# Four blocks of a product-key expert layer on one core: each block joins a running stream of the value table

## The chip, the cores and the metric

One core of one Trainium2 chip runs the whole program in one launch. The metric is device time in microseconds, the median of several runs. In what follows TensorE is the matmul engine (PE in the profile, PEld its weight loads), VectorE is DVE, ScalarE is ACT, GpSimd is POOL, and SyncE, which issues most transfers, is SP.

## The reference

One step of a decoder layer: 512 prompt tokens and 8 sample tokens go through two token mixers, then through a channel mixer with 16384 experts. The mixers are not touched by the change. The channel mixer is, for each block of 128 tokens:

```
q = (xb @ wq).reshape(blk, 8, 2, 128)
s = einsum('nhcd,ckd->nhck', q, subkeys)
s1, i1 = top_k(s[:, :, 0], 16);  s2, i2 = top_k(s[:, :, 1], 16)
cand = s1[..., :, None] + s2[..., None, :]
top_s, pos = top_k(cand, 16)
eidx = take_along_axis(i1 * 128 + i2, pos)
g = softmax(top_s)
act = gelu(einsum('nd,nhkd->nhk', xb, u[eidx]))
return einsum('nhk,nhkd->nd', g * act, v[eidx])
```

A token has 8 heads x 16 chosen experts = 128 experts. Each has one row of 1024 float32 numbers in `u` and one in `v`.

## The kernel before

The prompt is cut into four blocks of 128 tokens, here A0 and A1 (first half), B0 and B1 (second half). In the code and in the change's title they are blocks 1 to 4 or, as an index, 0 to 3. A half pass (the loop `for hf in range(2)`) does the mixers, the merge, and `scores`, which computes the scores of its two blocks and of the sample tokens. The channel mixer of A0 and A1 is worked off beside the second half pass, that of B0 and B1 behind it. A block goes through these steps:

- **Selection** (`topk`, `retrieve`, L973 to L1018): per head, VectorE's max, index and replace operations over scores, with small operations on GpSimd and ScalarE.
- **Gather** (`gather`, `gather_dot`, L1097 to L1109): 128 times GpSimd issues an indirect transfer (L1102) of 128 rows of `u`, one for each token, 128x1024; VectorE multiplies it with the tokens and sums along the row (L1108, "the dot"). Then `gelu_w` (L1122) makes the weights S.
- **One-hots** (`w_block`, L1154 to L1183): S becomes a dense matrix WT of 128 tokens x 16384 experts, written as 128 slices. In 32 groups of 4 tokens, VectorE compares (L1164, `ohe`), GpSimd multiplies by S (L1167, `oh`), VectorE may do some columns of that (L1169), ScalarE or VectorE make the second one-hot (L145 with L1174, L1177), TensorE multiplies (L1181, `ps_w`) and ScalarE copies the result into WT (L148). `ONAS` and `PMS` hold, per block, how many of the 4 second one-hots ScalarE makes and how many of the 4 products GpSimd makes.
- **Value stream** (`v_part`, L1273): the value table is read in 128 tiles of 128x1024 (L1275, on SP's queue, 5 buffers). For each tile and block TensorE does two matmuls of 512 columns (L1290), each two records in the trace.

A0 and A1 stream together through all 128 tiles, B0 joins for the last 28 (`JB = 100`) and then has 100 tiles of its own: 228 tile loads. B1 has no WT. Beside B0's own tiles `vg_run` gathers 128 rows of `v` for each of B1's tokens (L1313), and TensorE multiplies them with 32-column weights (L1318). The sample tokens (`sample_peer`, L1329 to L1373) are worked in steps: score load, lists, u rows, v rows. B0's gather is held until B1's selection has reached a given head (`HOLD`). A scheduler that reorders instructions on each engine sets the final order; program order is its starting point.

Of the kernel before, what the change touches and what calls it, by code (L numbers as in the profile page):

```python
# [15 lines left out]
P = 128  # L16
D = 1024
# [16 lines left out]
ONAS, PMS = (1, 4, 1, 0), (3, 2, 4, 4)  # L34
# [20 lines left out]
JH = 64  # L55
# [3 lines left out]
def step_kernel(  # L59
# [70 lines left out]
    def pst(tag):  # L130
        return ps.tile([P, 512], F32, tag=tag, name=f"ps_{tag}", bufs=PB[tag])
# [221 lines left out]
    def project(hf):  # L353
# [10 lines left out]
        xx = opnd(sp if hf else fa, f"x{hf}")  # L364
# [285 lines left out]
    nblk = 2  # L650

# [327 lines left out]
    def retrieve(pools, nb, s, rows, top, i12, eidx, vec=False):  # L979
# [23 lines left out]
        eq = (ring if nb[2] == "g" else sp).tile([P, 32, 16], F32, tag=nb[2], name="tk_eq", bufs=nb[3])[:rows]  # L1003
# [28 lines left out]
    def scores(hf, todo, xx):  # L1032
# [78 lines left out]
    def gather(hf, i):  # L1111
        sel, todo = halves[hf]
        d, tok = sel[i], todo[i][0]
        if i == 0 and HOLD[hf] is not None:
            hb, hh = divmod(HOLD[hf], 8)
            with tc.issue_after(sel[hb]["last", hh][HE].ins):
                gather_dot(d, tok, OFF[i])
        else:
            gather_dot(d, tok, OFF[i])
        gelu_w(d["S"], d["g"], d["S"], d["top"], d["e"].bitcast(F32))  # L1120
# [63 lines left out]

    halves = []
    xx, early = project(0), None
    for hf in range(2):
# [67 lines left out]

# [192 lines left out]
```

## Time and profile before

| | |
|---|---|
| Time before, three runs | 2279.82, 2296.55, 2286.86 us; median 2286.86 |
| The profiled execution | 2279.21 us; its span 2277.5 us |
| TensorE's mean granted clock | 0.949 of full speed |
| TensorE, VectorE, ScalarE, GpSimd busy | 92%, 62%, 26%, 58% of the span |
| DMA | 690.15 MB |

Busy is the share of the span in which an engine has an instruction running. The span's axis starts at its first instruction; all stretches are told on it. The second half's scoring fills about 1222 to 1336, A0 and A1 stream from about 1344, B0's one-hots fall in 1650 to 1800, and B0's own tiles with B1's gathered rows in 1930 to 2271.

### The profile page before, as it was taken

The page shows a single profiled execution, that of the slowest core. Times are in us where ns is not written, and L with a number is a line of the kernel's source. Part 1 is how long each engine was busy: PE and PEld are TensorE (multiplying, and loading weights), DVE is VectorE, ACT ScalarE, POOL GpSimd, SP SyncE. Part 2 cuts the span into 40 slices and gives each one's busy share as a digit, 9 for nine tenths or more (in the row PEclk, how much of TensorE's full clock was granted, in tenths as well). Part 3 has the DMA queues.
Part 4 walks back from the last instruction along what each step waited for, and adds up shares of the span by engine and source line. Part 5 has one row for each costly group of instructions (what it writes and reads, how often), then busy time and mean ns, then how long its engine had stood idle before and what let it go on. Part 6 is the DMA issues. An engine that isn't in the chain of part 4 may idle for free.

```text
span 2277.5 us, 26092 instructions
## 1 busy us (share of the span) xinstructions
PE 2098.4 (92%) x8208; PEld 1349.4 (59%) x8208; DVE 1403.7 (62%) x3382; ACT 593.5 (26%) x1615; POOL 1327.5 (58%) x1215
## 2 busy tenths in 40 slices
PE   6999899888999998998988866999999999899998
PEld 4776677777878776787766654444455544222233
DVE  1366675886799878767987989566388775000000
ACT  3334233312345323333423676000022100000000
POOL 0588773553586546667786778444278776555510
PEclk9999999989989999999998866999999999999999
DMA  5687676888799798999987147999699899999988
GB/s 161 198 269 236 229 239 229 282 297 287 243 329 324 269 321 321 337 369 313 318 311 245 43 167 248 410 409 409 252 365 355 320 403 362 410 407 409 409 332 284
DMA packets 293757, 690.15 MB, mean 303 GB/s; under 512 B 31054, under 2 KB 157066, under 8 KB 293618
## 3 DMA queue, kind: packets, MB, share of 16 engines
q0 software_dynamic: 112896, 411.09, 48.7%
q1 hardware_dynamic: 180722, 277.38, 35.1%
q8 instruction: 65, 1.06, 0.2%
q14 instruction: 74, 0.61, 0.1%
HBM read 670.19 MB, written 18.18 MB: 302 GB/s over the span
## 4 chain that ended last, share of the span: by engine, by line
PE 44%; DVE 11%; DMA 10%; issue 7%; POOL 5%; ACT 1%; DVEq 0%; POOLq 0%; ACTq 0%
PE y L1290 20%; PE ps_mm L288 9%; DMA vslab<-in_peer_v,vg_eT 6%; DVE urow L1108 3%; POOL urow L1102 3%; PE ps_mm L293 3%; PE y L1318 3%; PE ps_s L738 2%; DMA urow<-in_peer_u,k_e 1%; PE ps_w L1181 1%; POOL oh L1167 1%; PE ps_s L741 1%; DVE tk_w L975 1%; DVE ohe L1164 1%; DMA vpage<-in_cache_v,kidx 1%
## 5 line engine op out<-in xcount | busy, mean ns | idle before, releaser
L1102 POOL DMA_INDIRECT urow<-in_peer_u,k_e x512 | 632.2, 1235 | 326.9 <-DVE urow L1108 223.3
L1108 DVE SCALAR_TENSOR_TENSOR urow<-urow,xn 128x1024 f32<-128x1024 f32 x512 | 651.2, 1284 | 151.4 <-DMA urow<-in_peer_u,k_e 145.7
L1290 PE MATMUL y<-vtile,WT 128*128 128x512 f32 x1536 | 680.6, 598 | 3.0 <-DMA vtile<-in_peer_v 2.1
L1290 PEld LDWEIGHTS y<-vtile,WT 128*128 128x128 f32 x1536 | 286.6, 191 | 382.5 <-issue 377.8
L288 PE MATMUL ps_mm<-x,wch 128*128 128x264 f32 (+1 forms) x1536 | 385.9, 405 | 25.1 <-DVE sig L312 17.2
L288 PEld LDWEIGHTS ps_mm<-x,wch 128*128 128x128 f32 x1536 | 302.0, 201 | 81.5 <-DVE sig L312 20.7
L831 POOL TENSOR_TENSOR kpage<-kpage,qb 128x1024 f32<-128x1024 f32 x64 | 150.0, 2356 | 73.8 <-DMA qb<-scr_q 65.2
L288 PE MATMUL ps_mm<-hT,wch 128*128 128x256 f32 (+1 forms) x768 | 185.1, 391 | 0.7 <-DMA wch<-in_w_branch_b 0.5
L1313 POOL DMA_INDIRECT vslab<-in_peer_v,vg_eT x128 | 122.2, 955 | 106.2 <-DMA vslab<-in_peer_v,vg_eT 47.7
L1326 DVE TENSOR_TENSOR x1r<-x1r,y 128x512 f32<-128x512 f32 x8 | 5.2, 684 | 249.1 <-DMA x1r<-scr_x 238.3
L288 PEld LDWEIGHTS ps_mm<-hT,wch 128*128 128x128 f32 x768 | 144.4, 194 | 23.5 <-issue 1.3
L293 PE MATMUL ps_mm<-wch,x 128*128 128x256 f32 (+1 forms) x640 | 151.2, 388 | 0.3 <-DVE kS L690 0.3
L1318 PE MATMUL y<-vslab 128*32 128x512 f32 x512 | 138.6, 601 | 12.2 <-DMA vslab<-in_peer_v,vg_eT 12.2
L819 POOL DMA_INDIRECT vpage<-in_cache_v,kidx x64 | 79.8, 1248 | 106.6 <-DVE vacc L897 63.7
L1181 PE MATMUL ps_w<-oh,oh 128*128 128x128 f32 x512 | 88.3, 336 | 46.0 <-POOL oh L1167 29.2
L293 PEld LDWEIGHTS ps_mm<-wch,x 128*128 128x128 f32 (+1 forms) x640 | 108.3, 175 | 30.5 <-issue 2.8
L897 DVE SCALAR_TENSOR_TENSOR vacc<-vpage,aS,vacc 128x128 f32<-128x128 f32 x384 | 110.6, 359 | 19.4 <-DMA vpage<-in_cache_v,kidx 19.3
L1181 PEld LDWEIGHTS ps_w<-oh,oh 128*128 128x128 f32 x512 | 81.4, 242 | 62.3 <-POOL oh L1167 45.5
L1167 POOL TENSOR_TENSOR oh<-ohe,T_S 128x384 f32<-128x384 bf16 (+2 forms) x96 | 96.4, 1011 | 12.7 <-ACT T_S L148 5.6
L1318 PEld LDWEIGHTS y<-vslab 128*32 128x32 f32 x512 | 30.7, 109 | 112.0 <-issue 88.5
L832 DVE TENSOR_REDUCE sK<-kpage 128x16 f32<-128x1024 f32 x64 | 77.1, 1210 | 26.3 <-POOL kpage L831 26.2
L145 ACT ACTIVATE k_e<-k_top,zero 128x128 f32<-128x128 f32 x4 | 1.6, 402 | 346.0 <-DVE k_top L1126 346.0
(420 smaller groups left out, 2634.2 us busy)
## 6 DMA issues: line engine op xcount, KB each, us to landing
vtile<-in_peer_v SPq DMA_DIRECT2D x228, 512.0 KB
wch<-in_w_in SPq DMA_DIRECT2D x256, 256.0 KB
wch<-in_peer_wq SPq DMA_DIRECT2D x64, 256.0 KB
wch<-in_w_branch_a SPq DMA_DIRECT2D x32, 256.0 KB
wch<-in_w_branch_b SPq DMA_DIRECT2D x32, 256.0 KB
wch<-in_w_out SPq DMA_DIRECT2D x32, 256.0 KB
urow<-in_peer_u,k_e POOLq DMA_INDIRECT x512, 7.5
qb<-scr_q SPq DMA_DIRECT2D x8, 512.0 KB
```

Of the source, the lines that this page charges most:

```text
L288: nc.tensor.matmul(out, w[:, c0:c0 + m], xk[:, :n], start=(k == 0 and i == 0), stop=(k == KT - 1 and i == len(tt) - 1))
L293: nc.tensor.matmul(out, x[:, k, t0:t0 + m], ch[k // KP][:, k % KP, :n], start=(k == 0), stop=(k == KT - 1))
L819: nc.gpsimd.indirect_dma_start(out=t, out_offset=None, in_=rows, in_offset=bass.IndirectOffsetOnAxis(ap=kidx[:, b * 8 + pg:b * 8 + pg + 1] ...
L831: (nc.vector if KDV and pg % KDV == KDV - 1 else nc.gpsimd).tensor_mul(kt, kt, qb)
L897: nc.vector.scalar_tensor_tensor(acc[:, h, :], vt[:, h, :], wa, acc[:, h, :], op0=ALU.mult, op1=ALU.add)
L1102: nc.gpsimd.indirect_dma_start(out=gt, out_offset=None, in_=u_rows, in_offset=bass.IndirectOffsetOnAxis(ap=d["e"][:, k:k + 1], axis=0))
L1108: d["dot"] = nc.vector.scalar_tensor_tensor(gt, gt, 1.0, xn2, op0=ALU.mult, op1=ALU.mult, accum_out=d["S"][:, k:k + 1])
L1167: nc.gpsimd.tensor_mul(a[:, :PM], e.rearrange("p j t -> p t j")[:, :PM], sb[:, :PM])
L1181: nc.tensor.matmul(pw[:, t, :], b[:, t, :], a[:, t, :], start=True, stop=True)
L1290: nc.tensor.matmul(py[q], lw, rv[:, q * 512:(q + 1) * 512], start=(j == j0 and i == 0), stop=(j == j1 and i == len(pp) - 1))
L1313: nc.gpsimd.indirect_dma_start(out=gt, out_offset=None, in_=v_rows, in_offset=bass.IndirectOffsetOnAxis(ap=eT[:, t:t + 1], axis=0))
L1318: nc.tensor.matmul(py[q][32 * j:32 * j + 32, :], wz[:, t, :], gt[:, q * 512:(q + 1) * 512], start=(i == 0), stop=(i == 31), skip_group_che ...
```

## The change

- A0 streams alone through tiles 0 to 63, beginning inside the second half's scoring. For that the tiles and its accumulators have pools (`values`, `psumo`) that are open from there on, and the operands pool closes early.
- A1 joins for tiles 64 to 127. Then A1 goes on through tiles 0 to 63, B0 joins from tile 16 (`JC`), and goes on alone through tiles 64 to 127 and 0 to 15. That is 272 tile loads.
- `scores(1)` selects for B0 only; B1's selection is `late`, behind A0's one-hots. `HOLD` is not used any more. B0's gather follows.
- The sample block is done whole, between A0's end and B1's gather. Then B1's gather, then B0's one-hots.
- B1's value rows are gathered by expert slot: 128 transfers, one per slot with a row for each token (`v_rows_acc`), and VectorE multiplies each by its weight and adds it to the sum. TensorE's share of it (`vg_prep`, `vg_run`) is gone. The rows use 15 slots in the memory of A1's WT.
- Prompt results are stored from ScalarE's queue, not SP's.
- `ONAS[0]` goes from 1 to 2, `PMS[0]` from 3 to 4 and `PMS[1]` from 2 to 4.

```diff
-ONAS, PMS = (1, 4, 1, 0), (3, 2, 4, 4)
+ONAS, PMS = (2, 4, 1, 0), (4, 4, 4, 4)
-JH = 64
+JH, JC = 64, 16
...
-                if not BF[hf] or d is sel[0]:
+                if hf == 0 or d is sel[0]:
                     topk(d, h)
...
-        if BF[hf]:
+        def late():
             for h in range(8):
                 topk(sel[1], h)
-        for d, (tok, t0, rows, sample) in zip(sel, todo):
-            if not sample:
-                softmax16(tp, d["top"], d["g"], P, 8)
-        return sel
+            softmax16(tp, sel[1]["top"], sel[1]["g"], P, 8)
+        return sel, late
...
+    def v_done(tok, py):
+        t = dv[0].tile([P, D], F32, tag="v", name="x1r", bufs=VB)
+        nc.sync.dma_start(t, scr_x1[tok:tok + P])
+        for q in range(2):
+            nc.vector.tensor_add(t[:, q * 512:(q + 1) * 512], t[:, q * 512:(q + 1) * 512], py[q])
+        nc.scalar.dma_start(y_prompt[0, tok:tok + P], t)
+
+    def v_rows_acc(d, tok, acc, slot):
+        nc.sync.dma_start(acc, scr_x1[tok:tok + P])
+        for k in range(P):
+            gt = slot()
+            nc.gpsimd.indirect_dma_start(out=gt, out_offset=None, in_=v_rows,
+                                         in_offset=bass.IndirectOffsetOnAxis(ap=d["e"][:, k:k + 1], axis=0))
+            nc.vector.scalar_tensor_tensor(acc, gt, d["S"][:, k:k + 1], acc, op0=ALU.mult, op1=ALU.add)
+            yield
+        nc.scalar.dma_start(y_prompt[0, tok:tok + P], acc)
...
         if hf == 1:
+            octx.close()
+            dv[0] = ctx.enter_context(tc.tile_pool(name="values", bufs=1, side="right"))
             gather(0, 0)
             gather(0, 1)
+        sel, late = scores(hf, todo, xx2)
+        halves.append((sel, todo))
...
+            w_block(halves[0][0][0], wA0, wr, pst_w, 0)
+            late()
+            gather(1, 0)
+            useA0 = ([pst("a"), pst("o")], wA0, 0, P - 1)
+            for j in range(JH):
+                v_part(j, [useA0])
...
+    useA1 = (v_acc(1), wA1, JH, JH - 1)
+    for j in range(JH, P):
+        v_part(j, [useA0, useA1])
+    v_done(0, useA0[0])
+    steps = sample_peer()
+    for _ in steps:
+        pass
+    gather(1, 1, lambda: wr.tile([P, P], F32, name="ge_y", bufs=1))
+    wB0 = w_new(wr, wr)
+    w_block(selB[0], wB0, wr, pst_d, 2)
+    useB0 = (v_acc(2), wB0, JC, (JC - 1) % P)
     for j in range(JH):
+        v_part(j, [useA1] + ([useB0] if j >= JC else []))
+    v_done(P, useA1[0])
+    slab = [wt.tile([P, 8, D], F32, tag="WT", name="vslab", bufs=2) for _ in range(2)]
...
-        v_part(j, [useB0], False)
-        if j % 3 == 2:
+    run = v_rows_acc(selB[1], HALF + P, slab[0][:, 0, :], gslot)
+    for j in [*range(JH, P), *range(JC)]:
+        v_part(j, [useB0])
+        with tc.issue_after(selB[1]["rows"].ins):
             next(run, None)
```

VectorE, A1's first one-hots (L1164 before, L1171 after: `ohe`; `T_i` is A1's list). Before, they stand between the selections of the scoring (`tk_`, `k_top`):

```order
1415 L977 MAX_INDEX tk_si<-tk_sv,tk_w 128x8
1416 L973 MAX k_top<-tk_c 128x8
1417 L1164 TENSOR_TENSOR ohe<-iota_8781,T_i_10366 128x512 x3
1418 L1018 SCALAR_TENSOR_TENSOR k_e<-k_i_9320 128x16
1419 L973 MAX tk_sv<-sco 128x8 x2
1420 L1017 TENSOR_REDUCE k_i_9313<-tk_eq 128x2x16
1421 L974 MAX_INDEX tk_p<-k_top,tk_c 128x8
1422 L975 MATCH_REPLACE tk_w<-k_top,tk_c 128x136
1423 L975 MATCH_REPLACE tk_w<-tk_sv,sco 128x128
1424 L1169 TENSOR_TENSOR oh_10380<-ohe,T_S 128x256
```

After, four of them stand in B1's selection, and the next ones behind its last results (`k_i_8800` and `k_e` are B1's; `urow,k_S` are B0's dots):

```order
1470 L1033 TENSOR_TENSOR k_g<-smd,sml 128x128
1471 L1021 TENSOR_REDUCE k_i_8800<-tk_eq 128x2x16
1472 L1022 SCALAR_TENSOR_TENSOR k_e<-k_i_8800 128x16
1473 L1120 SCALAR_TENSOR_TENSOR urow,k_S<-urow,xn_10367 128x1024 x2
1474 L1021 TENSOR_REDUCE k_i_8800<-tk_eq 128x2x16
1475 L1337 MEMSET wz 128x64
1476 L1120 SCALAR_TENSOR_TENSOR urow,k_S<-urow,xn_10367 128x1024
1477 L1022 SCALAR_TENSOR_TENSOR k_e<-k_i_8800 128x16
1478 L1120 SCALAR_TENSOR_TENSOR urow,k_S<-urow,xn_10367 128x1024
1479 L1171 TENSOR_TENSOR ohe<-iota_9496,T_i_11036 128x512 x2
1480 L1120 SCALAR_TENSOR_TENSOR urow,k_S<-urow,xn_10367 128x1024
1481 L1171 TENSOR_TENSOR ohe<-iota_9496,T_i_11036 128x512
```

The fifth one-hot and all later ones have moved behind the end of B1's selection, each beside one dot of B0.

TensorE, B0's one-hots (`ps_w<-oh`) and the stream (`y`). Before, groups stand between stream matmuls:

```order
1347 L1290 MATMUL y_10959<-vtile,WT 128x512
1348 L1290 MATMUL y_10960<-vtile,WT 128x512
1349 L1181 MATMUL ps_w<-oh_12220,oh_12222 128x128 x4
1350 L1181 MATMUL ps_w<-oh_12235,oh_12237 128x128 x4
1351 L1290 MATMUL y_10961<-vtile,WT 128x512
1352 L1290 MATMUL y_10958<-vtile,WT 128x512
1353 L1290 MATMUL y_10959<-vtile,WT 128x512
1354 L1290 MATMUL y_10960<-vtile,WT 128x512
1355 L1290 MATMUL y_10961<-vtile,WT 128x512
1356 L1290 MATMUL y_10958<-vtile,WT 128x512
```

After, the stream's last matmuls of A1 are followed by all 32 groups (8 shown):

```order
1470 L1198 MATMUL y_11596<-vtile,WT 128x512
1471 L1148 MATMUL ps_w<-ident,k_S 128x128
1472 L1198 MATMUL y_11595<-vtile,WT 128x512
1473 L1198 MATMUL y_11596<-vtile,WT 128x512
1474 L1188 MATMUL ps_w<-oh_12566,oh_12568 128x128 x4
1475 L1188 MATMUL ps_w<-oh_12581,oh_12583 128x128 x4
1476 L1188 MATMUL ps_w<-oh_12596,oh_12598 128x128 x4
1477 L1188 MATMUL ps_w<-oh_12611,oh_12613 128x128 x4
1478 L1188 MATMUL ps_w<-oh_12626,oh_12628 128x128 x4
1479 L1188 MATMUL ps_w<-oh_12641,oh_12643 128x128 x4
1480 L1188 MATMUL ps_w<-oh_12656,oh_12658 128x128 x4
1481 L1188 MATMUL ps_w<-oh_12671,oh_12673 128x128 x4
```

The stream matmuls between the groups are gone; the next stream matmul comes after the 32nd group.

SP's queue, the sample's requests (`s`, `scr_g`, `scr_e`, `gT`, `eT`) among the value tiles. Before:

```order
280 L1275 DMA vtile<-in_peer_v 128x1024 x70
281 L1331 DMA s_11743<-scr_s 64x256
282 L1275 DMA vtile<-in_peer_v 128x1024 x3
283 L1099 DMA xn_11805<-scr_xn_59 128x1024
284 L1275 DMA vtile<-in_peer_v 128x1024 x2
285 L1338 DMA scr_g<-s_g 64x16
286 L1275 DMA vtile<-in_peer_v 128x1024
287 L1344 DMA gT<-scr_g 128x8x1
288 L1275 DMA vtile<-in_peer_v 128x1024 x2
289 L1337 DMA scr_e<-s_e 64x16
290 L1275 DMA vtile<-in_peer_v 128x1024 x2
291 L1343 DMA eT<-scr_e 128x8x1
```

After:

```order
297 L1194 DMA vtile<-in_peer_v 128x1024 x97
298 L1311 DMA s_11986<-scr_s 64x256
299 L1194 DMA vtile<-in_peer_v 128x1024 x4
300 L1110 DMA xn_12150<-scr_xn_59 128x1024
301 L1194 DMA vtile<-in_peer_v 128x1024 x2
302 L1318 DMA scr_g<-s_g 64x16
303 L1194 DMA vtile<-in_peer_v 128x1024
304 L1324 DMA gT<-scr_g 128x8x1
305 L1317 DMA scr_e<-s_e 64x16
306 L1202 DMA x1r<-scr_x_58 128x1024
307 L1323 DMA eT<-scr_e 128x8x1
```

The score load `s` has moved from behind the 70th tile load to behind the 121st, and the list `eT` from behind the 80th to behind the 128th. The residual load `x1r` of A0 has come among them.

## Rows read from the trace of the kernel before

**Rows 1.** Page, engines: busy us (share), instructions; DMA total; the value-tile issues.

```profile
PE 2098.4 (92%) x8208; PEld 1349.4 (59%) x8208; DVE 1403.7 (62%) x3382; ACT 593.5 (26%) x1615; POOL 1327.5 (58%) x1215
...
DMA packets 293757, 690.15 MB, mean 303 GB/s; under 512 B 31054, under 2 KB 157066, under 8 KB 293618
...
vtile<-in_peer_v SPq DMA_DIRECT2D x228, 512.0 KB
```

**Rows 2.** Windows: length, then PE, PEld, DVE, ACT, POOL busy (instructions), PEclk, DMA share, GB/s.

```profile
1222.00:1304.00 82.00, 75.47 (x367) 59.97 (x365) 70.24 (x382) 36.55 (x101) 50.44 (x88) 0.96 0.36 120
...
1336.00:1413.00 77.00, 48.09 (x196) 37.54 (x196) 63.49 (x112) 52.61 (x153) 66.44 (x59) 0.63 0.77 267
1413.00:1612.00 199.00, 198.29 (x465) 88.69 (x466) 118.76 (x195) 3.14 (x11) 91.18 (x93) 0.99 1.01 400
...
1672.00:1800.00 128.00, 126.31 (x472) 70.55 (x470) 115.95 (x174) 34.52 (x115) 106.47 (x87) 1.00 0.95 346
...
1930.00:2194.00 264.00, 250.60 (x762) 69.53 (x760) 10.48 (x31) 1.20 (x4) 133.31 (x140) 0.99 1.02 406
```

**Rows 3.** Windows, a stretch inside the first common stream.

```profile
1450.00:1600.00 150.00, 150.00 (x351) 66.43 (x350) 91.16 (x148) 0.00 (x0) 68.46 (x74) 1.00 1.03 409
```

**Rows 4.** Chain that ended last, in order: start us, us, what.

```profile
1425.53 232.88 PE y L1290 x542
...
2194.04 72.31 PE y L1290 x168
2266.37 4.50 DMA x1r<-scr_x
```

**Rows 5.** Timeline of POOL: start us, us, instruction [idle before].

```profile
1336.77 1.56 POOL L1102 DMA_INDIRECT urow<-in_peer_u,k_e  x1 [0.15 <-issue]
1338.64 0.94 POOL L1102 DMA_INDIRECT urow<-in_peer_u,k_e  x1 [0.30 <-issue]
```

**Rows 6.** Groups by form, 1230 to 1345, DVE's selection: busy us, mean ns | idle.

```profile
L976 DVE MAX8 tk_sv<-tk_w 128x8 f32<-128x128 f32 x32 | 8.9, 277 | 0.0
...
L1017 DVE TENSOR_REDUCE k_i<-tk_eq 128x32 f32<-128x512 f32 x15 | 10.0, 666 | 0.0
```

**Rows 7.** Groups by form, 1336 to 1413, A1's one-hots.

```profile
L145 ACT ACTIVATE oh<-iota,T_n 128x128 f32<-128x128 f32 x84 | 26.9, 398 | 0.0
...
L1174 ACT ACTIVATE oh<-oh,one 128x512 f32<-128x512 f32 x23 | 16.1, 716 | 0.1
L148 ACT ACTIVATE WT<-ps_w 128x256 f32<-128x256 f32 x46 | 15.1, 380 | 21.5 <-PE ps_w L1181 21.4
```

**Rows 8.** Groups by form, 1413 to 1612, B0's gather.

```profile
L1108 DVE SCALAR_TENSOR_TENSOR urow<-urow,xn 128x1024 f32<-128x1024 f32 x95 | 116.1, 1225 | 78.4 <-DMA urow<-in_peer_u,k_e 78.4
L1102 POOL DMA_INDIRECT urow<-in_peer_u,k_e x93 | 91.2, 980 | 96.9 <-DVE urow L1108 90.6 <-issue 5.7 <-DVE ohe L1164 0.3
```

**Rows 9.** Groups by form, 1650 to 1805, B0's one-hots beside B1's gather.

```profile
L1108 DVE SCALAR_TENSOR_TENSOR urow<-urow,xn 128x1024 f32<-128x1024 f32 x70 | 92.6, 1351 | 10.5 <-DMA urow<-in_peer_u,k_e 10.3
L1102 POOL DMA_INDIRECT urow<-in_peer_u,k_e x68 | 89.7, 1319 | 25.2 <-DVE urow L1108 14.3 <-issue 8.6 <-DVE oh L1177 1.0
...
L1167 POOL TENSOR_TENSOR oh<-ohe,T_S 128x512 f32<-128x512 bf16 x32 | 34.2, 1081 | 6.2 <-ACT T_S L148 5.6 <-PE ps_w L1181 0.2
...
L1177 DVE TENSOR_TENSOR oh<-iota,T_i 128x384 f32<-128x384 f32 x29 | 27.7, 969 | 2.8 <-PE ps_w L1181 2.6 <-ACT oh L145 0.2
...
L1164 DVE TENSOR_TENSOR ohe<-iota,T_i 128x512 bf16<-128x512 bf16 x29 | 18.0, 628 | 16.6 <-POOL oh L1167 16.6
```

**Rows 10.** Groups by form, 1930 to 2194, B1's gathered value rows.

```profile
L1318 PE MATMUL y<-vslab 128*32 128x512 f32 x512 | 138.6, 601 | 12.2 <-DMA vslab<-in_peer_v,vg_eT 12.2
L1313 POOL DMA_INDIRECT vslab<-in_peer_v,vg_eT x128 | 122.2, 955 | 106.2 <-DMA vslab<-in_peer_v,vg_eT 47.7 <-PE y L1318 22.6 <-issue 20.7
```

**Rows 11.** Timeline of SP's queue, the sample's requests: start us, us, instruction.

```profile
1632.46 0.45 SPq L1331 DMA_DIRECT2D s<-scr_s  x1
...
1666.66 0.43 SPq L1343 DMA_DIRECT2D eT<-scr_e  x1
```

More of the change, by code (lines that the diff above doesn't have):

```diff
@@ L130, in pst @@
     def pst(tag):
-        return ps.tile([P, 512], F32, tag=tag, name=f"ps_{tag}", bufs=PB[tag])
+        return (pso if tag in "ao" else ps).tile([P, 512], F32, tag=tag, name=f"ps_{tag}", bufs=PB[tag])
     def st1(shape, name, dt=F32):
@@ L1054, in score @@
                 for c in range(2):
-                    nc.tensor.matmul(p[:rows, c * P:(c + 1) * P], qts[c][:, t0:t0 + rows], skT[:, c, :],
-                                     start=True, stop=True)
+                    mm = nc.tensor.matmul(p[:rows, c * P:(c + 1) * P], qts[c][:, t0:t0 + rows], skT[:, c, :],
+                                          start=True, stop=True)
+                if d is not None:
+                    d["score"] = mm
                 if sample:
@@ L1109, in gather_dot, with gather @@
                                                           accum_out=d["S"][:, k:k + 1])
-    def gather(hf, i):
+    def gather(hf, i, y=None):
         sel, todo = halves[hf]
         d, tok = sel[i], todo[i][0]
[L1114 to L1120, printed above, removed]
+        gather_dot(d, tok, OFF[i])
+        gelu_w(d["S"], d["g"], d["S"], d["top"], d["e"].bitcast(F32) if y is None else y())
     def gelu_w(s, g, out, t, y):
@@ L1183, in w_block, with v_part @@
                 copy(w[:, :, t0:t0 + TG], pw[:, :, j0:j0 + w.shape[1]].rearrange("p t j -> p j t"))
+    def v_part(j, use):
+        vt = dv[0].tile([P, D], F32, tag="v", name="vtile", bufs=VB)
+        nc.sync.dma_start(vt, v_rows[j * P:(j + 1) * P])
+        for py, wT, j0, j1 in use:
+            w = next(w[:, j - b, :] for w, b in wT if b <= j < b + w.shape[1])
+            for q in range(2):
+                nc.tensor.matmul(py[q], w, vt[:, q * 512:(q + 1) * 512], start=(j == j0), stop=(j == j1))
+    def v_done(tok, py):
+        t = dv[0].tile([P, D], F32, tag="v", name="x1r", bufs=VB)
+        nc.sync.dma_start(t, scr_x1[tok:tok + P])
+        for q in range(2):
+            nc.vector.tensor_add(t[:, q * 512:(q + 1) * 512], t[:, q * 512:(q + 1) * 512], py[q])
[5 more added lines that the diff above has]
+            nc.gpsimd.indirect_dma_start(out=gt, out_offset=None, in_=v_rows,
+                                         in_offset=bass.IndirectOffsetOnAxis(ap=d["e"][:, k:k + 1], axis=0))
+            nc.vector.scalar_tensor_tensor(acc, gt, d["S"][:, k:k + 1], acc, op0=ALU.mult, op1=ALU.add)
+            yield
+        nc.scalar.dma_start(y_prompt[0, tok:tok + P], acc)
     halves = []
@@ L1254, in step_kernel @@
     fctx.close()
+    tctx.close()
     dctx = ExitStack()
```

113 lines of the change are left out of this document (19 added, 94 removed).

## The prediction

> **What bounds the kernel now.** I read the page's engines first [rows 1]. TensorE is busy 92% of the span of 2277.5 us, no other engine over 62%. That is an average, so the windows of the tail come next [rows 2]. Three kinds of stretch show. From 1336 to 1413 TensorE is busy 48.09 of 77 us at a granted clock of 0.63 (of 2.4 GHz): it waits for A1's one-hots. From 1413 to 1612 and in the 150 us of [rows 3] it is full, and the DMA share is 1.01 to 1.03 at 400 to 409 GB/s: engine and memory are both at their limit. From 1930 to 2194 the share is 1.02 again, TensorE busy 250.60 of 264. The chain [rows 4] says the same: 542 records of the value stream in 232.88 us, then 168 in 72.31, 0.43 us each. One block's share of a tile is two matmuls in four records, 1.71 us; two blocks, 3.42 us. A value tile and a gathered row set are each 128x1024 float32, 0.524 MB; at 409 GB/s that is 1.28 us. So a one-block tile with one gathered row costs DMA 2.56 us and TensorE 1.71: that pair is DMA-bound, while two blocks per tile (3.42) cover it.
>
> **The change part by part.** The times below are on the axis of the profiled execution; everything up to the second half's scoring is untouched.
>
> *What TensorE gains and DMA loses.* The 512 records of gathered rows on TensorE go: 138.6 us [rows 10]. The 1536 records of the stream stay. Value tiles go from 228 [rows 1] to 64 + 64 + 64 + 80 = 272: 44 more, 23 MB beside 690 MB, 44 x 1.28 = 56 us at the limit. The 128 v rows stay, loaded by expert slot instead of by token.
>
> *(a) Scoring.* A0's stream starts inside it: the order has about 10 tiles before the last scoring matmul, 10.5 x 1.71 = 18 us on a TensorE that is busy 75.47 of 82 us there [rows 2], so they lengthen it. For block A0 VectorE loses its column of one-hot products and a third of its compares; this may give back 5 us, bounds 0 to 15. Against that the hold is gone which let B0's gather start at 1336.77 [rows 5], where the last tenth or so of B1's selection before that point no longer stands. B0's first row: 1324, bounds 1310 to 1338.
>
> *(b) B1's selection.* In the new order VectorE places only four of A1's 32 first one-hots before the rest of B1's selection. What is left is 6.5 heads. A head is ten operations over 128 columns at 0.277, five over 136 at about 0.29, a reduce at 0.666 [rows 6] and small ones, 6 to 6.4 us: 41 us. With it stand 27 dots of B0, 1.225 to 1.35 us [rows 8, 9] and 0.08 for reading the accumulator: 38. With one-hots and a softmax about 84 us, at 90% filled 93 (the row before has VectorE busy 63.49 of 77 us with a lighter mix). A1's one-hots go on at about 1424, bounds 1395 to 1445. The stream of A0 alone covers TensorE for part of this.
>
> *(c) A1's one-hots.* 28 groups are left. ScalarE per group, by busy time over count [rows 7]: 4 x 0.32 + 0.70 + 2 x 0.33 = 2.64 us, some 2.7 with gaps. GpSimd now multiplies all four columns, 1.08 [rows 9], and issues one row, 0.94 + 0.30 idle [rows 5]: 2.3. ScalarE sets the pace: 28 x 2.7 = 76 to 78, at worst the 3.35 us a group that 23 groups took in those 77 us: 94. A0 and A1 can stream together from 1502, bounds 1470 to 1525. A0's 64 lone tiles have run out by then, so TensorE idles some 45 us.
>
> *(d) A0 and A1 together:* 64 x 3.42 = 219 us, to 1721. DMA needs 64 tiles and some 70 rows, 172 us: hidden.
>
> *(e) The sample block.* Its requests stand in SP's queue behind value tiles. Before, the score load went at 1632.46, behind the 70th tile, and the expert list 34 us later [rows 11], and nothing hung on them. Now they stand behind the 121st and the 128th, and all of the sample's work ends before B0's one-hots begin on TensorE. Tile 121 is let in when tile 116 has been used: 1502 + 52 x 3.42 = 1680; the list 27 later; eight u rows and dots and the gelu another 35 to 40: 1745. TensorE has work meanwhile, 21 tiles of A1 alone (36 us) and the sample's 14, until the transposes for B0 at 1779: 8 us of stall beyond the work, bounds 0 to 30.
>
> *(f) B0's one-hots.* Now 32 groups stand on TensorE with no stream matmul between, so their whole pace is exposed. GpSimd: 32 x 1.08 + 49 rows x 1.4 + about 5 = 108; VectorE: 32 x (0.63 + 0.97) + 49 x 1.43 = 121 at the durations of [rows 9], 98 at uncontended ones. I take 115, as the two engines share the load as they did then, bounds 95 to 135. TensorE does only some 30 us of work in it, DMA only 54 pieces (69 us of 115). B0 streams from 1894. Before, stream matmuls between the groups hid this: from 1672 TensorE was busy 126.31 of 128 us [rows 2].
>
> *(g) The rest.* By then 153 tiles are loaded, so 119 remain, with 69 u rows and 128 v rows: 316 x 1.28 = 405 us, bounds 405 to 420, to 2306. TensorE's need is 91 x 1.71 and 71 x 1.71, 277 us: it is hidden behind DMA. The accumulate on VectorE is not in this trace. Its nearest row is the dot of the same shape, 1.225 us [rows 8]; a row issue is 0.955 [rows 10]. Both lie under 2.56 us per pair, so I add nothing, with a high end in the last rival and none below, since DMA alone sets the low one. How tile and row share the engines decides only which finishes first.
>
> The Trainium skill, "DMA: Bandwidth & Descriptors", section "SWDGE vs HWDGE vs iDMA", says that each DMA engine takes turns between the queues that software and hardware descriptors feed. By that rule tiles and rows would advance one for one and both end together. This trace doesn't settle it, as [rows 10] show row issues waiting for buffers; the total is the same either way.
>
> *(h) Tail.* Before, the chain's last load ended at 2270.87 [rows 4] and the span at 2277.5: the adds and the store took some 6.5 us, and as much is added here. The last store goes out from ScalarE's queue; nothing else is on it by then, 0 to 2 us either way. Early pools, operands in their own pool and own PSUM banks cost no instruction; their price is the waits in (b) and (c).
>
> Sum: 2306 + 6.5 = 2313 of span, and 1.7 around it (2279.21 less 2277.5) gives 2314, 1.5% above 2279.21. The median of the runs, 2286.86, stands 0.3% above the profiled execution; on that scale I say 2318.
>
> A check by bytes: from the first B0 row on there are 400 row sets and 228 tiles before, 628 x 1.28 = 805 us, of 935 that passed; 130 us idle. After: 400 and some 253, 837 us, and idle in (b) to (f) of 37 + 47 + 0 + 46 = 130. The change must find 32 us of DMA idle to break even; it starts only 12 earlier.
>
> **The rivals.**
>
> *Faster: A1's one-hots are not held up.* If VectorE clears B1's selection by 1380, because the topk's waits were TensorE's and ScalarE's and not its own, A0 and A1 join at 1425 instead of 1502, and B0's start falls to about 1817. The end is then 1817 + 405 + 8 = 2230 to 2245, 1.8% faster. For it: A1's one-hots ran to 1413 before, with B1's selection done. Against: selection and dots alone are 79 us of VectorE. It decides when the join comes before about 1445.
>
> *No change.* Every stall in (c), (e) and (f) a little shorter: B0's one-hots at uncontended pace (95 instead of 115), the join at 1487. That is 35 us, ending near 2278. For it: each is inside its own bounds. Against: the contended durations in [rows 9] were measured with the same neighbours.
>
> *Slower by more: the accumulate locks out row issues.* If issue (0.94 + 0.30) and accumulate (1.225) can't overlap, a row costs 2.47 us. When A1's stream ends, about 121 v rows and 75 tiles are left; the rows then take 299 us, where DMA needs 196 x 1.28 = 251 for both: 48 later, 2362. For it: rows issued at 1320 ns beside one-hots and dots [rows 9]. Against: 980 ns beside dots alone [rows 8].
>
> The Trainium skill, "SBUF — State Buffer", section "Who interferes with whom", says that VectorE and GpSimd share a port pair that is locked exclusively. By it this rival would get more weight; the 980 ns of [rows 8] beside 95 dots don't agree with a lock for each row's issue.
>
> **How the numbers follow.** Forecast 0.50, no change 0.26, faster 0.17, slower by more 0.07. A measurement tells about 1% from no change here, 23 us: below 2264 is faster, above 2310 slower. The forecast's own spread (2295 to 2340) gives 0.41 to slower and 0.09 to same; no change gives 0.24 to same, 0.02 to slower. That makes 0.17 faster, 0.33 same, 0.50 slower. The range runs from 2240, in the middle of the faster rival, to 2348; it leaves out half of that rival and the last one. The likeliest case's own range is 2295 to 2340.
>
> **What would show it.** Right: TensorE idle for tens of us before A0 and A1 stream together at about 1500; a stretch of some 115 us near 1780 with the B0 one-hots on TensorE at low clock; then a DMA share of 1.0 to the end, with TensorE waiting for value tiles. Wrong: a join before 1445, one-hots of B0 in under 90 us, or an end stretch where VectorE or GpSimd, not DMA, ends the waits.

## The result, and the profile after

The changed kernel takes 2351.44 us (median of four runs, 2339.56 to 2355.60) against 2291.70 beside it: a ratio of 1.026, 95% interval 1.0211 to 1.0309. It is slower, as forecast, but by 2.6%, where 2318 was named and 2348 was the end of the range. The profiled execution took 2339.56 us, its span 2337.9.

The page of the changed kernel, engines, transfers, the two groups of B1's value rows and the value-tile issues; compare [rows 1] and [rows 10]:

```profile
PE 1982.6 (85%) x7694; PEld 1318.8 (56%) x7694; DVE 1551.5 (66%) x3440; ACT 612.5 (26%) x1647; POOL 1348.2 (58%) x1216
...
DMA packets 300090, 713.16 MB, mean 305 GB/s; under 512 B 31758, under 2 KB 157770, under 8 KB 299954
...
L1213 DVE SCALAR_TENSOR_TENSOR vslab<-vslab,k_S 128x1024 f32<-128x1024 f32 x128 | 164.5, 1285 | 56.8 <-DMA vslab<-in_peer_v,k_e 53.7
L1211 POOL DMA_INDIRECT vslab<-in_peer_v,k_e x128 | 152.2, 1189 | 86.2 <-DMA vslab<-in_peer_v,k_e 53.5
...
vtile<-in_peer_v SPq DMA_DIRECT2D x272, 512.0 KB, 6.8
```

TensorE's work fell by 115.8 us and its share from 92% to 85%. 713.16 - 690.15 = 23.0 MB more are moved: 44 tile loads. The accumulate took 1.285 us a row, as the dots do.

Windows of the changed kernel, the columns as in [rows 2]: up to the join of A0 and A1, the common stream, the sample block, B0's one-hots, B0 with A1, and then three pieces of the end:

```profile
1320.00:1478.00 158.00, 111.81 (x427) 63.67 (x427) 117.06 (x333) 90.03 (x258) 136.46 (x140) 0.87 0.87 315
1478.00:1693.00 215.00, 214.75 (x507) 95.33 (x506) 105.05 (x199) 4.26 (x11) 80.16 (x86) 1.00 0.90 346
1693.00:1766.00 73.00, 59.46 (x120) 18.99 (x119) 17.53 (x41) 1.20 (x4) 22.41 (x21) 0.91 0.93 354
1766.00:1888.00 122.00, 66.53 (x268) 53.81 (x267) 116.80 (x171) 42.95 (x130) 103.03 (x87) 0.60 0.74 234
1901.00:2047.00 146.00, 145.82 (x340) 64.71 (x341) 79.40 (x129) 0.00 (x0) 67.59 (x68) 1.00 1.03 410
2047.00:2180.00 133.00, 103.78 (x209) 35.97 (x207) 76.62 (x69) 1.60 (x4) 77.21 (x56) 0.99 1.03 409
2180.00:2276.00 96.00, 0.00 (x0) 0.00 (x0) 92.96 (x73) 0.00 (x0) 66.50 (x65) 0.51 0.96 377
2276.00:2334.00 58.00, 51.85 (x116) 22.65 (x116) 1.21 (x2) 0.00 (x0) 0.00 (x0) 0.92 0.80 281
```

The common stream fills TensorE (214.75 of 215) but not DMA (0.90). Around the one-hots of B0 neither is full. From 1901 to 2180 DMA is at 409 to 410 GB/s. The row from 2180 is the one to stop at: TensorE is busy 0.00 of 96 us, and there are still value tiles to come, as the last row shows (116 records, 29 tiles).

SP's waits in the last 440 us (engine and line, what it waited for, us in total, times, longest):

```profile
SPq L1194 <- PE y L1198: 253.7, 113, 3.8
SPq L1194 <- DMA out_y_prompt<-vslab: 111.1, 1, 111.1
```

One value-tile load waits 111.1 us for `out_y_prompt<-vslab`, the store of B1's result, which is issued from ScalarE's queue and can only run when the last of 128 rows is accumulated. TensorE's timeline there (start, us, instruction, idle before):

```profile
2172.48 1.98 PE L1198 MATMUL y<-vtile,WT 128*128 128x512 f32 x4 [0.58 <-DMA vtile<-in_peer_v]
...
2177.60 1.98 PE L1198 MATMUL y<-vtile,WT 128*128 128x512 f32 x4 [0.58 <-DMA vtile<-in_peer_v]
2281.58 18.81 PE L1198 MATMUL y<-vtile,WT 128*128 128x512 f32 x39 [102.00 <-DMA vtile<-in_peer_v]
```

Up to 2177.60 a tile comes every 2.56 us. Then TensorE waits 102.00 us for one. VectorE's timeline beside it:

```profile
2175.41 1.28 DVE L1213 SCALAR_TENSOR_TENSOR vslab<-vslab,k_S 128x1024 f32<-128x1024 f32 x1 [1.27 <-DMA vslab<-in_peer_v,k_e]
2177.84 22.42 DVE L1213 SCALAR_TENSOR_TENSOR vslab<-vslab,k_S 128x1024 f32<-128x1024 f32 x17 [1.15 <-DMA vslab<-in_peer_v,k_e]
```

With tiles running it gets one row in 2.56 us; when they stop, its accumulates stand back to back, 17 in 22.42 us, so that now VectorE sets the pace, at 1.32 us a row (busy 92.96 of 96 us). The rows are done at 2275. Then the store goes out, the tiles come back, and 29 of them run alone at TensorE's pace.

Why would a tile load wait for a store from another engine's queue? The program's order, with the semaphores that each instruction waits for, says it (first the store on ScalarE, then tile loads on SP; `...` where rows are left out):

```
1389 L1215 DMA out_y_prompt<-vslab 128x1024 [waits DMAHW7_49,DVE_49]
...
857 L1194 DMA vtile<-in_peer_v 128x1024 [waits DMAHW0_49,PE_49]
858 L1194 DMA vtile<-in_peer_v 128x1024 [waits DMAHW1_49,PE_49]
859 L1194 DMA vtile<-in_peer_v 128x1024 [waits DMAHW7_49,DMAHW2_49,PE_49]
860 L1194 DMA vtile<-in_peer_v 128x1024 [waits DMAHW3_49,PE_49]
```

Transfers issued from SP and from ScalarE signal their end on the same eight semaphores, given out in turn by the scheduler. The store got number 7. The next load to get number 7 is row 859, with 28 more behind it, and it must wait until the store has signalled. No data passes between the two. Transfers issued from GpSimd have eight semaphores of their own.

Two more views answer to rows of before. B0's first u row (timeline of GpSimd) and the sample's score load and list (SP's queue), against [rows 5] and [rows 11]:

```profile
1320.38 1.04 POOL L1113 DMA_INDIRECT urow<-in_peer_u,k_e  x1
```

```profile
1659.19 0.45 SPq L1311 DMA_DIRECT2D s<-scr_s  x1
...
1686.76 0.37 SPq L1323 DMA_DIRECT2D eT<-scr_e  x1
```

And B0's one-hots, groups by form from 1766 to 1888, against [rows 9]:

```profile
L1120 DVE SCALAR_TENSOR_TENSOR urow<-urow,xn 128x1024 f32<-128x1024 f32 x54 | 73.3, 1379 | 0.0
L1113 POOL DMA_INDIRECT urow<-in_peer_u,k_e x55 | 67.7, 1231 | 18.6 <-DVE urow L1120 7.7 <-issue 7.6 <-DVE oh L1184 0.9
...
L1174 POOL TENSOR_TENSOR oh<-ohe,T_S 128x512 f32<-128x512 bf16 x32 | 37.2, 1165 | 0.7
L1184 DVE TENSOR_TENSOR oh<-iota,T_i 128x384 f32<-128x384 f32 x32 | 28.9, 914 | 0.0
L1171 DVE TENSOR_TENSOR ohe<-iota,T_i 128x512 bf16<-128x512 bf16 x32 | 21.8, 689 | 5.7 <-POOL oh L1174 3.8 <-ACT T_i L151 1.9
```

GpSimd's products (1165 ns) and the dots (1379) are a little slower than they were with the same neighbours (1081 and 1351), and GpSimd and VectorE are busy 103 and 117 of the 122 us.

**The balance of transfers.** The stretch from B0's first row to the last value matmul, before and then after:

```profile
1337.00:2271.00 934.00, 888.56 (x2523) 384.28 (x2522) 410.35 (x705) 98.89 (x304) 506.21 (x462) 0.97 0.95 362
```

```profile
1320.00:2334.00 1014.00, 765.71 (x2007) 360.57 (x2006) 613.28 (x1025) 140.71 (x409) 563.92 (x527) 0.87 0.91 344
```

934 us at 362 GB/s are 338 MB, 827 us at the 409 GB/s of [rows 3]; 1014 at 344 are 349 MB, 853 us. So 26 of the 80 us more are transfers, and idle DMA time went from 107 to 161. The same sum over the windows above puts that at 36 us up to the join, 33 in the common stream, 10 beside the sample block, 52 beside B0's one-hots, and 26 from 2180 on. The first four are 131; the prediction had counted 130 for all. The last was not in it.

That balance starts at B0's first row, and by then the changed kernel has already loaded 24 tiles, beside the scoring. From the last residual store ahead of the scoring to the last value matmul, in both kernels, the sums are 357.0 MB in 1083.1 us before and 380.1 MB in 1149.2 after: 56 us more of transfers at 409 GB/s, the price of the 44 loads, and idle DMA time up only from 210 to 220. The early tiles fill DMA time that stood idle, and the new stalls and the store wait take it back.

### The profile page after: what moved, and what is told of

Read it like the earlier page. It is cut to its first block, busy times and chain, and to the rows that moved or that the text cites. A ratio compares the mean times of both kernels' runs of the same rounds, so it can differ in the third digit from the quotient of the medians.

```text
span 2337.9 us, 25323 instructions
## 1 busy us (share of the span) xinstructions
PE 1982.6 (85%) x7694; PEld 1318.8 (56%) x7694; DVE 1551.5 (66%) x3440; ACT 612.5 (26%) x1647; POOL 1348.2 (58%) x1216
## 2 busy tenths in 40 slices
DMA packets 300090, 713.16 MB, mean 305 GB/s; under 512 B 31758, under 2 KB 157770, under 8 KB 299954
## 4 chain that ended last, share of the span: by engine, by line
PE 43%; DVE 15%; DMA 10%; POOL 5%; issue 5%; ACT 1%; POOLq 0%; DVEq 0%; ACTq 0%; SPq 0%
PE y L1198 14%; PE ps_mm L291 10%; DMA vslab<-in_peer_v,k_e 5%; DVE urow L1120 4%; DVE vslab L1213 4%; PE ps_a L1198 3%; PE ps_mm L296 3%; PE ps_o L1198 3%; POOL urow L1113 3%; DMA vtile<-in_peer_v 2%; PE ps_w L1188 1%; DMA vpage<-in_cache_v,kidx 1%; POOL oh L1174 1%; DMA urow<-in_peer_u,k_e 1%; PE ps_s L742 1%
## 5 line engine op out<-in xcount | busy, mean ns | idle before, releaser
L1113 POOL DMA_INDIRECT urow<-in_peer_u,k_e x512 | 600.9, 1174 | 382.5 <-DVE urow L1120 273.6
L1120 DVE SCALAR_TENSOR_TENSOR urow<-urow,xn 128x1024 f32<-128x1024 f32 x512 | 663.1, 1306 | 162.1 <-DMA urow<-in_peer_u,k_e 157.0
L1198 PE MATMUL y<-vtile,WT 128*128 128x512 f32 x1024 | 476.2, 609 | 145.8 <-DMA vtile<-in_peer_v 145.3
L1198 PEld LDWEIGHTS y<-vtile,WT 128*128 128x128 f32 x1024 | 191.9, 193 | 417.3 <-issue 220.7
L1213 DVE SCALAR_TENSOR_TENSOR vslab<-vslab,k_S 128x1024 f32<-128x1024 f32 x128 | 164.5, 1285 | 56.8 <-DMA vslab<-in_peer_v,k_e 53.7
L1211 POOL DMA_INDIRECT vslab<-in_peer_v,k_e x128 | 152.2, 1189 | 86.2 <-DMA vslab<-in_peer_v,k_e 53.5
L1198 PE MATMUL ps_a<-vtile,WT 128*128 128x512 f32 x256 | 134.4, 607 | 2.0 <-DMA vtile<-in_peer_v 1.4
L1198 PE MATMUL ps_o<-vtile,WT 128*128 128x512 f32 x256 | 132.1, 598 | 0.0
L1174 POOL TENSOR_TENSOR oh<-ohe,T_S 128x512 f32<-128x512 bf16 x96 | 109.5, 1147 | 5.3 <-PE ps_w L1188 1.8
L993 POOL TENSOR_TENSOR tk_c<-tk_sv 128x120 f32<-128x120 f32 (+1 forms) x33 | 19.2, 582 | 115.1 <-DVE tk_sv L980 105.2
```

The lines of the kernel that those rows point to most:

```text
L1113: d["rows"] = nc.gpsimd.indirect_dma_start(out=gt, out_offset=None, in_=u_rows, in_offset=bass.IndirectOffsetOnAxis(ap=d["e"][:, k:k + 1], ...
L1120: d["dot"] = nc.vector.scalar_tensor_tensor(gt, gt, 1.0, xn2, op0=ALU.mult, op1=ALU.mult, accum_out=d["S"][:, k:k + 1])
L1174: nc.gpsimd.tensor_mul(a[:, :PM], e.rearrange("p j t -> p t j")[:, :PM], sb[:, :PM])
L1198: nc.tensor.matmul(py[q], w, vt[:, q * 512:(q + 1) * 512], start=(j == j0), stop=(j == j1))
L1211: nc.gpsimd.indirect_dma_start(out=gt, out_offset=None, in_=v_rows, in_offset=bass.IndirectOffsetOnAxis(ap=d["e"][:, k:k + 1], axis=0))
L1213: nc.vector.scalar_tensor_tensor(acc, gt, d["S"][:, k:k + 1], acc, op0=ALU.mult, op1=ALU.add)
```

## The experiments

The part of the program that the change leaves alone varies by up to 34 us between runs: its last residual store came at 1184.8 us in one profile and at 1218.5 in another. So single runs are compared by what is left of the span after that store, called the tail here: 1089.6 us before, 1153.1 after. Each tail is from one profile. In the six kernels that are alike up to B0's stream, that stream begins 702.3 to 705.5 us after the store, so a difference of 3 us or less says nothing.

| kernel | tail, us | ratio to before, 95% interval |
|---|---|---|
| changed | 1153.1 | 1.0260 (1.0211 to 1.0309) |
| store from GpSimd's queue | 1133.4 | 1.0191 (1.0146 to 1.0236) |
| stores from SP's queue | 1155.0 | 1.0265 (1.0223 to 1.0306) |
| store on SP behind the last tile | 1134.2 | one run |
| GpSimd's store, B0 joins at 0 | 1141.9 | 1.0244 (1.0198 to 1.0289) |
| GpSimd's store, B0 joins at 48 | 1150.8 | 1.0264 (1.0217 to 1.0310) |
| GpSimd's store, a quarter of the accumulate | 1130.7 | one run |
| GpSimd's store, half the last tile loads | 1083.2 | one run |
| GpSimd's store, B0's compares on ScalarE | 1155.9 | 1.0304 (1.0253 to 1.0356) |
| before, B1's rows on VectorE | 1076.7 | 0.9908 (0.9875 to 0.9940) |
| the same, with the change's one-hot split | 1069.4 | 0.9937 (0.9904 to 0.9970) |

### The store of B1's rows from GpSimd's queue

```diff
-        nc.scalar.dma_start(y_prompt[0, tok:tok + P], acc)
+        nc.gpsimd.dma_start(y_prompt[0, tok:tok + P], acc)
```

> One edit to the changed kernel: the store of B1's accumulated rows goes out from GpSimd's queue instead of ScalarE's. Theory S (store wait): in the changed kernel's trace one value-tile load on SP waits 111 us for that store, so no tile comes from 2180 to 2276 and 29 tiles at TensorE's 1.71 us are left behind the rows. Without the wait tiles and rows run out together or rows last: at 2180 some 30 tiles and 73 rows are left, 103 x 1.28 = 132 us, end of the stream at about 2312 and a span of about 2317 instead of 2338; no value-tile load waits for a store. Rival R (rest bound by transfers and VectorE whatever the order): the wait only changes which of them is late, span 2333 to 2343.

Measured: a span of 2323.1 and a tail of 1133.4, 19.7 us less than the changed kernel's. Its end in windows:

```profile
1905.00:2051.00 146.00, 145.96 (x340) 64.71 (x341) 79.97 (x131) 0.00 (x0) 69.23 (x68) 1.00 1.03 410
2051.00:2258.00 207.00, 159.98 (x325) 54.93 (x323) 112.88 (x97) 1.60 (x4) 117.02 (x85) 1.00 1.03 409
```

Tiles now run to 2258 at 409 GB/s and the rows alone end it. B0's stream began 705 us after the last residual store in both, so all of the 19.7 lies at the end: that is the store wait, as theory S has it. Whole times agree, but are not clear of noise by themselves: the intervals of the two ratios overlap a little. The span came 6 above the expected 2317, 5 of it from the later start of this run (its last residual store came at 1189.7, against 1184.8).

### All prompt stores from SP's queue

```diff
-        nc.scalar.dma_start(y_prompt[0, tok:tok + P], t)
+        nc.sync.dma_start(y_prompt[0, tok:tok + P], t)
...
-        nc.scalar.dma_start(y_prompt[0, tok:tok + P], acc)
+        nc.sync.dma_start(y_prompt[0, tok:tok + P], acc)
```

> One part of the change undone: all prompt stores go out from SP's queue, as before the change. In the order the store of B1's rows stands 38 tile loads before the end of SP's queue. Theory S: the load behind the store waits for it in the queue itself, so the rows end near 2270 with some 38 to 40 tiles left, 39 x 1.71 = 67 us: span 2340 to 2352, no better than the changed kernel. Rival R: 2333 to 2343. If ScalarE's queue itself were what costs (the idea that the queue is bad), the span would fall to 2315 or less.

Measured: span 2353.8, tail 1155.0. Undoing this part brings nothing back: SP itself now stands at the store for longer, with tile loads behind it.

```profile
SPq L1215 <- DVE vslab L1213: 116.6, 1, 116.6
```

### The store on SP, behind the last tile load

```diff
-        nc.scalar.dma_start(y_prompt[0, tok:tok + P], acc)
+        with tc.issue_after(last_tile_load.ins):
+            nc.sync.dma_start(y_prompt[0, tok:tok + P], acc)
```

> Spans are now counted from the last store of a residual row block ahead of the second half's scoring, since the part before it, which the change leaves alone, varies by 19 us between runs (before: 2277.5 - 1187.9 = 1089.6; changed: 2337.9 - 1184.8 = 1153.1; store from GpSimd's queue: 1133.4). One edit to the changed kernel: the last store goes out from SP's queue, queued behind the last value-tile load. Theory S (a tile load that must wait for that store costs the time, whichever queue it is on): 1130 to 1138. Rival (SP's or ScalarE's hardware queue itself is slower for the store than GpSimd's): 1150 or more.

Measured: 1134.2. The same queue for this store as in the run before, 20.8 us less: it is the place of the store ahead of tile loads that costs, not the queue. (The run before had also moved the other prompt stores to SP; up to B0's stream that changed nothing, 705.5 us against 705.2.) The reading rests on the tail alone: this run's whole time, 2349.36 us, is that of the changed kernel, since its last residual store came 29 us later. B0's stream began 2.9 us earlier after that store than in the changed kernel, so 16 of the 18.9 us lie in the end.

### B0 joins at tile 0, and at tile 48

```diff
-JH, JC = 64, 16
+JH, JC = 64, 0
```

> On top of the store from GpSimd's queue, B0 joins the second pass at tile 0 instead of 16: 256 tile loads instead of 272, 8.4 MB less, and 16 lone tiles of A1 (27 us of TensorE) less ahead of B0's one-hots. Theory B (transfers bind from A0's end on): 16 x 1.28 = 20 us less, as far as no more DMA idle time comes: span 2295 to 2305. Rival C (what binds is TensorE without cover while the sample block and B0's one-hots are worked): nothing is gained, B0's stream starts where it did, 2312 to 2325.

Measured: a tail 8.5 us longer than with 16, though 16 tiles fewer are loaded; the ratios' intervals overlap. Both theories miss it. B0's stream did start 16 us earlier after the last residual store, but the end took 24 us more. GpSimd's group of value rows from 1893 to 2110 shows why:

```profile
L1211 POOL DMA_INDIRECT vslab<-in_peer_v,k_e x18 | 20.9, 1163 | 56.4 <-PE y L1198 46.3 <-DVE vslab L1213 5.9 <-issue 3.7
```

Row issues stood 46.3 us behind `PE y`. All but seven of the slots for the rows are memory of A1's WT, so they wait for A1's last tile. With a common pass of 64 two-block tiles instead of 48 that comes 40 us later, counted from the last residual store, and from 1893 to 2105 DMA runs at 362 GB/s; with 16 that wait was 7.8 us in all, and DMA at 410.

> On top of the store from GpSimd's queue, B0 joins the second pass at tile 48: 304 tile loads, 16.8 MB more, and the order puts 20 lone tiles of A1 among B0's one-hot groups. Theory B: 32 more tiles cost 41 us of DMA, of which the 52 us of DMA idle beside B0's one-hots take up 26 to 41: span 2315 to 2335, not faster than JC = 16. Rival C: the cover is worth its own time, 20 x 1.71 = 34 us less: span about 2283.

Measured: 17.4 us longer than with 16. 32 tiles are 41 us of transfers; so some 24 were taken up by idle time, just below the least that theory B gave (26). Rival C is out: B0's stream did start 24 us earlier, but the order puts only 25 of B1's u rows among the one-hot groups where there were 49, and those rows and the extra tiles had to be loaded all the same.

### A quarter of the accumulate

```diff
-            nc.vector.scalar_tensor_tensor(acc, gt, d["S"][:, k:k + 1], acc, ...)
+            nc.vector.scalar_tensor_tensor(acc[:, 0:256], gt[:, 0:256], d["S"][:, k:k + 1], acc[:, 0:256], ...)
```

> On top of the store from GpSimd's queue, VectorE accumulates only the first 256 of the 1024 columns of each of B1's value rows (three quarters of that sum are left out). Rival of the prediction (row issue and accumulate can't overlap, 2.47 us a row): 121 rows get about 0.9 us shorter each, 1133 - 60 to 100 = 1035 to 1075. Theory B (the pair of tile and row costs 2.56 us of transfers): rows and tiles still go at 2.56, and the lone rows at 1.28 instead of 1.30: 1125 to 1135.

Measured: 1130.7, 2.7 less, which is within the noise of the tail. Beside tiles a row still takes 2.56 us, so the accumulate is not what a row waits for there. It does lengthen the row issues on GpSimd (their median falls from 1430 to 939 ns in this run), but the tail shows no price for that. Only the lone rows change: from 2260 to 2310 they went at 1.28 us and 403 GB/s in this run, where the full accumulate, busy 48.29 of 50 us there, held them to 1.32 us and 389 GB/s.

### Half the tile loads of the last loop

```diff
-        v_part(j, [useB0])
+        vt = v_part(j, [useB0], vt if j % 2 else None)
```

> On top of the store from GpSimd's queue, the last loop loads only every second of its 80 value tiles and uses each twice (the other 40 tiles are left out): 21 MB less, the same matmuls, the same rows. Theory B: 40 x 1.28 = 51 us less transfer in a stretch that has nothing else to wait for; after A1's end 80 tile uses x 1.71 = 137 us of TensorE and 121 rows x 1.28 = 155 are the next bounds, so 1082 to 1095. Rival (rows are bound by GpSimd or VectorE): 1125 to 1135.

Measured: 1083.2, 50.2 less for 40 loads, 1.26 us for each. After A1's end:

```profile
1930.00:2090.00 160.00, 159.56 (x372) 70.41 (x371) 87.70 (x146) 1.60 (x4) 77.69 (x78) 1.00 1.02 408
2090.00:2210.00 120.00, 120.00 (x281) 53.19 (x280) 79.13 (x62) 0.00 (x0) 79.67 (x58) 1.00 1.03 409
```

With two tile uses to a load, TensorE is full again (120.00 of 120) while DMA stays at 409. Counted from B0's stream, which began 0.9 us earlier here, it is 49.3 us, 1.23 for each. The stretch is bound by transfers as the prediction had it, and a tile load there costs nearly the 1.28 us that was put down for it.

### B0's compares on ScalarE

```diff
-ONAS, PMS = (2, 4, 1, 0), (4, 4, 4, 4)
+ONAS, PMS = (2, 4, 4, 0), (4, 4, 4, 4)
```

> On top of the store from GpSimd's queue, ScalarE makes all four of B0's second one-hots (ONAS[2] from 1 to 4), so VectorE loses 32 x 0.97 = 31 us of the 117 us that it is busy in the 122 us of B0's one-hots. Theory D (VectorE, with its dots, sets the pace of that stretch): the stretch falls to GpSimd's pace, about 103 to 108 us, and the dots and rows that run on fill DMA: 1115 to 1122. Rival G (GpSimd's products and row issues set it): 1130 to 1136.

Measured: 22.5 us longer, outside both. The scheduler, with VectorE freer, put 64 of B1's row issues among the one-hot groups where it had put 49, and the stretch grew to 161 us at GpSimd's pace (141 of 161 us busy):

```profile
L1113 POOL DMA_INDIRECT urow<-in_peer_u,k_e x75 | 106.4, 1418 | 19.6 <-issue 15.3 <-PE ps_w L1188 1.8 <-DVE urow L1120 1.8
...
L1174 POOL TENSOR_TENSOR oh<-ohe,T_S 128x512 f32<-128x512 bf16 x32 | 35.3, 1105 | 0.6
```

Which engine would set the pace with the order unchanged stays open.

### The kernel before, with B1's rows on VectorE

```diff
-    yB1 = v_acc(0)
-    run = vg_run(vg_prep(selB[1], dp, ...), yB1, slots)
+    run = v_rows_acc(selB[1], HALF + P, slab[0][:, 0, :], slots)
     for j in range(JB):
         v_part(j, [useB0], False)
-        if j % 3 == 2:
-            next(run, None)
+        next(run, None)
```

with the store queued behind the last tile load, as above.

> One part of the change alone, on the kernel before: B1's value rows are gathered by expert slot into 15 slots and accumulated on VectorE (no matmuls for them), with the store queued on SP behind the last value tile; the streams, their 228 tile loads and the order ahead of them stay as before. Before, the end had TensorE and DMA both full until 2194 (rows on TensorE) and then 45 lone tiles at TensorE's 1.71 us with DMA at 288 GB/s. Theory B (only transfers bind the end, once TensorE is freed of 138 us): 1930 to 2271 moved 107.2 + 22.2 MB, 316 us at 409 GB/s instead of 341, so 20 to 25 us less: from the last residual store 1064 to 1072, ratio to before 0.988 to 0.993. Rival (the part costs what the whole change does, since VectorE's accumulate and the row issues hold each other up): 1090 or more, ratio 1.00 or more.

Measured: ratio 0.9908 (0.9875 to 0.9940), 0.9% less than the kernel before and clear of 1. The end of the kernel before, and then of this one:

```profile
2194.00:2271.00 77.00, 77.00 (x181) 34.08 (x180) 0.02 (x1) 0.00 (x0) 0.00 (x0) 1.00 0.83 288
```

```profile
1930.00:2180.00 250.00, 146.24 (x293) 50.00 (x292) 149.94 (x144) 2.07 (x7) 159.31 (x127) 0.86 1.02 406
2180.00:2262.00 82.00, 68.88 (x147) 25.72 (x145) 29.74 (x25) 0.00 (x0) 20.99 (x15) 1.00 0.95 362
```

DMA is at 406 GB/s from 1930 and still at 362 after 2180, where the kernel before had 288 from 2194 on. The tail, 1076.7, is 5 above what was expected; B0's first row came 4 us later in this run.

> The run before this one with the change's split of the one-hots as well: ONAS[0] from 1 to 2, PMS from (3, 2, 4, 4) to (4, 4, 4, 4). If VectorE sets the pace of the scoring and of A1's one-hots (busy 63.49 of 77 us, GpSimd 66.44), taking a part of both from it brings the first row of B0 and the join forward by 5 to 10 us: 1056 to 1066. If GpSimd sets it, 128 to 256 columns more a group cost 32 x 0.25 to 0.5 = 8 to 16 us: 1075 to 1085.

Measured: tail 1069.4, with B0's first row 8 us earlier than in the run before it, but a ratio of 0.9937 (0.9904 to 0.9970). The tail lies between the two forecasts, and the two ratios' intervals overlap; whether the split helps is not settled.

## Why the prediction missed

*(a) to (f) held, in part by luck.* B0's first row was put at 1324 and came at 1320.4; the join at 1502, came at 1480; A0's end 1721, was 1698; B0's transposes 1779, was 1767; B0's one-hots 115 us, were 122; B0's stream 1894, was 1890. (Two of the windows above were cut 2 and 5 us early.) The join came 22 us early, inside its bounds: A1's one-hots went on at 1410, not 1424, and 28 groups took 70 us, 2.5 each, where 2.7 was taken. The sample block then took 69 us where 58 was put down, as TensorE waited for tiles seven times, 13.5 us in all, while the sample's requests stood among them. That and the longer one-hots nearly cancelled the early join. The reason in (a) was half wrong: the hold held nothing, since every engine's order in the kernel before is the same without it. B0's first row came 13 us earlier, counted from the last residual store; the split of the one-hots alone brought 8 of them.

*(g) held in its law, and was a little short in its count.* Tiles and rows went at 1.28 us each, in pairs of 2.56; the halved loads show it. With the store out of the way the end takes 428 us (1894.8 to 2323.1). The sum had 418: the middle of its 405 to 420, and 6.5. The bytes moved are 325 pieces, not 316: only 149 tile loads had been issued by then, not 153, and the residual loads and result stores were not counted. The lone rows at the very end ran below 409 GB/s, at the pace of VectorE's accumulate, for which (g) had added nothing; that cost some 2 us.

*(h) is the step that failed.* "The last store goes out from ScalarE's queue; nothing else is on it by then, 0 to 2 us either way." The queue was empty, but the store was not alone: it shares completion semaphores with SP's tile loads, and in the scheduler's order the load that takes its semaphore next has 28 more behind it. That cost 19.7 us by one repair and 18.9 by the other, 16 of these in the end itself. The forecast span of 2313, with 20 for the store, 10 from (g) and 4 less for the earlier start of B0's stream, is 2339; 2337.9 was measured.

The rest of the miss is the step from the span to the median. The median was put 4 us above the profiled execution, though 0.3% of 2314 is 8; here it lay 12 above, as that of the kernel before beside it did (2291.70 against 2279.21).

The check by bytes did not bear out the sum, either: 1324 + 837 + 130 + 6.5 is a span of 2298, 15 short of 2313, and the prediction did not take that up. Measured were 853 us of transfers and 161 idle.

*The signs.* TensorE stood idle 46 of the 158 us before the join, and B0's one-hots took 122 us at a granted clock of 0.60, as forecast. A DMA share of 1.0 lasted only to 2180. Behind that the sign of being wrong came: VectorE, not DMA, set the pace of the lone rows, and then TensorE that of the lone tiles.

*The rivals.* "Faster" needed a join before 1445; it came at 1480. "No change" needed stalls 35 us shorter; those of the forecast's list were as long as listed. "Slower by more" came near in time (2362) but not in cause: row issues do get longer beside the accumulate, yet with a quarter of the accumulate the tail is 2.7 us shorter, not 60.

The sentence on turns between queues can now be checked: the Trainium skill, "DMA: Bandwidth & Descriptors", section "SWDGE vs HWDGE vs iDMA", has each DMA engine take turns between software and hardware descriptors, and here tiles (hardware) and rows (software) went one for one, each every 2.56 us from 2075 to 2178. The trace agrees.

**What the change comes to.** Freeing TensorE of B1's rows pays: alone it gives 0.9%, since at the end before, TensorE and DMA were both full. Streaming A0 alone early, with the order that goes with it, does not: it costs 44 tile loads where transfers bind. The nearest comparison is the last run, which has the change's one-hot split too: from its tail (1069.4) to that with the store from GpSimd's queue (1133.4) it is 64 us. By the bytes that the two moved in it, 357.0 and 379.5 MB, 55 of them are transfers, and some 9 more idle DMA time. That sum fits, but no run took the extra loads away from the change and left all else: the one that joined B0 at tile 0, with 16 loads fewer, ran into waits for row slots.

## What to carry to other kernels

Where engine and DMA are both full, take work from the engine without adding bytes: moving 128 row sets from TensorE to VectorE gained 0.9%, re-reading 23 MB to keep TensorE busy came with a larger loss. When idle time of two kernels is compared, start both sums at a point that the change leaves alone. Before a store or load is moved to another engine's queue, list the semaphores of the program's order: a transfer that must wait long for its data holds up whatever takes the same semaphore next, here on another engine's queue. A transfer that ends last belongs behind the last load of its queue, or on a queue that shares no semaphore with the stream.

## What the hardware showed that was not expected

The untouched first half of the program took between 1184.8 and 1218.5 us in profiles of kernels that are alike there, nearly 3%, more than most of the effects measured here. And the row issues on GpSimd took half as long again beside VectorE's accumulate (median 1430 ns, 939 with a quarter of it) without any effect on the time, while the same accumulate, at 1.32 us a row against 1.28 of DMA, became the limit as soon as rows ran without tiles.
